# A two-layer streaming encoder on one core: Strassen's seven products for part of the second channel MLP

## The chip, the core and the metric

The kernel runs on one core of a Trainium2 chip. Its time is the device time of one execution in microseconds (us). Five engines work from queues of their own, each in order: TensorE (PE, with its weight loads PEld), VectorE (DVE), ScalarE (ACT), GpSimd (POOL) and SyncE (SP), which here issues nearly all DMAs.

## The reference

1024 prompt rows and 32 sample rows of 1024 channels go through two layers. Each layer has a mixer (a spatial gating unit in layer 0, a pooling mixer in layer 1) and a channel MLP (called the FFN), with an RMSNorm in front of and behind each of them and a modulation by the conditioning vectors (adaLN, "ada" in the kernel):

```
for i in range(DEPTH):                                  # 2 layers
    mod = silu(c) @ w_ada[i] + b_ada[i]
    sh1, sc1, gt1, sh2, sc2, gt2 = split(mod, 6)
    h = rmsnorm(x, g_norm[i, 0]) * (1 + sc1) + sh1
    mix = sgu_mixer(h) if i == 0 else pool_mixer(h)
    x = x + gt1 * rmsnorm(mix, g_norm[i, 1])
    h = rmsnorm(x, g_norm[i, 2]) * (1 + sc2) + sh2
    f = square(relu(h @ ffn_w_up[i])) @ ffn_w_down[i]   # 1024 -> 4096 -> 1024
    x = x + gt2 * rmsnorm(f, g_norm[i, 3])
```

All is float32. The pool mixer takes trailing means over 2, 4, 8 and 16 rows in four groups of 256 channels and multiplies each group with a 256 x 256 matrix.

## The kernel before

**Layout.** Channels lie on the partitions, in eight blocks of 128 (KB); rows are columns. The columns form three tiles: tiles 0 and 1 of 384 prompt rows, tile 2 of 256 prompt and 32 sample rows (288). `acc[t]` holds a tile's residual stream or the sum in the making, `hh[t]` and `hl[t]` its modulated input.

**Products.** Every factor is split into a high part and the rest: `wh` and `wl` for weights, `hh` and `hl` for the input, `fh` and `fl` for the hidden activations. A product is three matmuls, wh x hh, wh x hl and wl x hh (lines 847, 848 and 849). The split of a loaded weight block of 128 x 1024 is a copy on ACT (`wh`, line 404) and a difference on DVE (`wl`).

**The FFN.** It goes by chunks of 512 hidden channels, eight in a layer. One `ffn_item` is a chunk for one tile: four up blocks `pf` of 24 matmuls each, relu and square on ACT, the split into `fh` and `fl`, and later eight down blocks `pg` of 12 matmuls, each added into `acc[t]` by DVE. Part of the next item's up blocks goes ahead of the down part (`pending`, `flush`), so that TensorE has work while the hidden activations are made. `passes` (lines 305 to 312) lists the order: (layer, chunk, tiles that share the loaded weights). In layer 1 it is tile 0's chunks 0 to 3, tile 1's, tile 2's, then chunks 4 and 5 for all three, 6 and 7 for tiles 0 and 1, and 6 and 7 for tile 2.

**Weights.** One list, `stream`, holds all loads in order: weights and, between them, the pieces of `w_ada` (`some_ada`), whose sums DVE forms (`do_ada`, the tile aa). Each load lands in one of three `raw` buffers (line 377 issues it on SP), is split into two of sixteen slots, and a slot is free once its block has been used for the last time.

**The chain of a tile between the layers.** It is a generator, called a filler, whose steps `weave` puts between the blocks of the FFN, by a running count of TensorE's and DVE's time (`time["pe"]`, `time["dve"]`); `finish` forces what is left. In `to_pool` for tile t: the residual behind layer 0 (`residual`, with the tile re-read from DRAM as `xo_r` and stored again in `xd`), the norm and modulation, the window sums of the pool mixer (`win`), the products with its four matrices (`wg` loads, `pp` at line 1672, two blocks a group, copied into `acc[t]` by ACT and squared), the statistics (a matmul with ones, `pn`, then a reciprocal square root with one correction step: `sc`, `sm`, `r`, `q`), the residual behind the mixer (`mix_to_ffn`), its statistics, and the modulation: in `apply` DVE scales `acc[t]` in place, ACT writes `hh[t]` and DVE `hl[t]`. Names end with the tile in the code (`r_rp` of tile 1, `r_1x`), buffer numbers are left out in the profile. `run_ffn` calls `finish` on a tile's filler ahead of its chunk 0.

**The end.** `to_out` makes a tile's last residual, turns it by DVE transposes into `turned`, and stores it in 32 DMAs, 24 on SP and 8 on POOL.

Of the kernel before, what the change touches and what calls it, by code (L numbers as in the profile page):

```python
# [15 lines left out]
P = 128  # L16
D = 1024
KB = D // P
# [10 lines left out]
W_SLOTS = 16  # L29
RAW_SLOTS = 3  # L30
# [4 lines left out]
def tile_stream_encoder_step(  # L35
# [83 lines left out]
    vd = dram.tile([SEQ + DEC, SGU], F32, name="vd")  # L119

# [235 lines left out]
    wpos = {k: i for i, k in enumerate(worder)}  # L356
    wdone = set()
# [43 lines left out]
    def do_w(key, r):  # L401
# [4 lines left out]
        tt(out=wl, in0=r, in1=wh.bitcast(F32), op=ALU.subtract)  # L406

# [141 lines left out]
    def stream_ready():  # L549
        k = state["next"]  # L550
        if k >= len(stream):
            return False
        if stream[k][0] == "w":
            i = wpos[stream[k][1]] - W_SLOTS // 2
            return i < 0 or worder[i] in wdone
        return True

    def stream_step():
# [6 lines left out]
        if kind == "w":  # L565
            do_w(key, r)
        elif kind == "wide":
# [17 lines left out]
    def stream_waits():  # L585

        kind, key = stream[state["next"]][:2]
        if kind == "w":
# [834 lines left out]
    def ffn_item(p, t, after):  # L1423
# [88 lines left out]
    def mix_to_ffn(st, l):  # L1512
# [8 lines left out]
        yield from modulate(out[0], l, 2, 3)  # L1521
# [292 lines left out]
```

## Time and profile before

| | |
|---|---|
| Median of three runs | 2161.54 us (2161.33 to 2162.09) |
| The profiled execution | 2161.22 us |
| its span, first to last instruction | 2159.4 us |
| DVE busy | 1429.8 us (66%) |
| ACT busy | 971.0 us (45%) |
| POOL busy | 15.3 us (1%) |
| DMA, read and written | 312.96 MB, mean 145 GB/s |

The page is of the profiled execution. Busy times are the union of an engine's instructions, weight loads (PEld) overlap the matmuls. Durations of consecutive instructions of one engine can overlap, so the pace of a run of equal instructions is read from their starts. In rows of the timeline the first number is the start, the second the time, and "x2" says that two instructions in a row were joined. A matmul's name for its product is the tile that it writes (pf: up, pg: down, pp: pool mixer, pn: statistics).

### The profile page before, as it was taken

The numbers are of one execution on the slowest core, as the hardware profiler recorded it, in microseconds if no ns is written. First come the engines' busy times: TensorE is split into PE (matmuls) and PEld (weight loads), VectorE is DVE, ScalarE is ACT, GpSimd is POOL, SyncE is SP. The second block draws the span as 40 slices with busy tenths as digits, with TensorE's granted clock in tenths as the row PEclk, the third lists the DMA queues.
The fourth block names the chain that finished last, engine by engine and source line by source line (L and its number), as shares of the span: only waits on it lengthen the run. The fifth ranks groups of instructions, "written<-read, shape, count | busy, mean of one in ns | idle before, by whom it ended". The sixth has DMA issues, their size and how long they took to land.

```text
span 2159.4 us, 33252 instructions
## 1 busy us (share of the span) xinstructions
PE 2145.1 (99%) x13233; PEld 2076.5 (96%) x13233; DVE 1429.8 (66%) x2496; ACT 971.0 (45%) x1644; POOL 15.3 (1%) x34
## 2 busy tenths in 40 slices
PE   9999999999999999999999999999999999999998
PEld 6778999999999999999999999999999999999998
DVE  6787738457778549486757879869675554523377
ACT  5534322233456652323445566666554542313354
POOL 0000000000000000000000000000000000000001
PEclk9999999999999999999999999999999999999999
DMA  8487524253447454244645466565455552302255
GB/s 307 147 263 215 168 82 132 84 163 102 135 125 221 127 156 147 79 136 127 184 127 162 145 186 191 156 202 155 142 169 150 162 152 64 104 14 79 70 138 127
DMA packets 383152, 312.96 MB, mean 145 GB/s; under 512 B 39475, under 2 KB 346203, under 8 KB 382997
## 3 DMA queue, kind: packets, MB, share of 16 engines
q1 hardware_dynamic: 382324, 309.95, 47.5%
q8 instruction: 103, 1.69, 0.3%
q0 software_dynamic: 640, 0.88, 0.1%
q14 instruction: 53, 0.43, 0.1%
q10 hardware_dynamic: 32, 0.01, 0.0%
HBM read 278.95 MB, written 31.84 MB: 144 GB/s over the span
## 4 chain that ended last, share of the span: by engine, by line
PE 96%; DVE 2%; DMA 1%; ACT 1%; issue 0%; DVEq 0%; SPq 0%
PE pg L847 11%; PE pf L847 11%; PE pf L849 11%; PE pf L848 11%; PE pg L848 11%; PE pg L849 11%; PE po L847 3%; PE po L848 3%; PE po L849 3%; PE pu L847 3%; PE pu L849 3%; PE pu L848 3%; PE pv L874 2%; PE pv L875 2%; PE pv L876 2%; PE psp L1353 1%
## 5 line engine op out<-in xcount | busy, mean ns | idle before, releaser
L847 PE MATMUL pg<-fh,wh_dn 128*128 128x384 f32 (+1 forms) x1536 | 495.8, 323 | 0.0
L847 PE MATMUL pf<-hh,wh_up 128*128 128x384 f32 (+1 forms) x1536 | 494.4, 322 | 0.0
L848 PE MATMUL pf<-hl,wh_up 128*128 128x384 f32 (+1 forms) x1536 | 493.1, 321 | 0.0
L849 PE MATMUL pf<-hh,wl_up 128*128 128x384 f32 (+1 forms) x1536 | 492.9, 321 | 0.2 <-DVE wl_up L79 0.2
L848 PE MATMUL pg<-fl,wh_dn 128*128 128x384 f32 (+1 forms) x1536 | 492.6, 321 | 0.5 <-DVE fl L79 0.5
L849 PE MATMUL pg<-fh,wl_dn 128*128 128x384 f32 (+1 forms) x1536 | 492.5, 321 | 0.0
L79 DVE TENSOR_TENSOR wl_up<-raw,wh_up 128x1024 fp32r<-128x1024 f32 x152 | 185.5, 1221 | 164.5 <-ACT wh_up L404 164.5
L848 PEld LDWEIGHTS pg<-fl,wh_dn 128*128 128x128 f32 x1536 | 288.3, 188 | 1.6 <-DVE fl L79 0.8
L847 PEld LDWEIGHTS pg<-fh,wh_dn 128*128 128x128 f32 x1536 | 288.3, 188 | 1.5 <-ACT fh L1260 0.6
L849 PEld LDWEIGHTS pf<-hh,wl_up 128*128 128x128 f32 x1536 | 288.6, 188 | 0.5 <-DVE wl_up L79 0.5
L848 PEld LDWEIGHTS pf<-hl,wh_up 128*128 128x128 f32 x1536 | 288.3, 188 | 0.4
L847 PEld LDWEIGHTS pf<-hh,wh_up 128*128 128x128 f32 x1536 | 288.2, 188 | 0.4
L849 PEld LDWEIGHTS pg<-fh,wl_dn 128*128 128x128 f32 x1536 | 288.3, 188 | 0.0
L404 ACT ACTIVATE wh_up<-raw 128x1024 fp32r<-128x1024 f32 x152 | 161.2, 1060 | 278.2 <-PE pf L848 212.2
L79 DVE TENSOR_TENSOR acc<-acc,pg 128x384 f32<-128x384 f32 (+1 forms) x336 | 173.6, 517 | 146.9 <-PE pg L849 146.4
L404 ACT ACTIVATE wh_dn<-raw 128x1024 fp32r<-128x1024 f32 x152 | 160.8, 1059 | 204.0 <-PE pg L848 169.9
L79 DVE TENSOR_TENSOR wl_dn<-raw,wh_dn 128x1024 fp32r<-128x1024 f32 x152 | 185.7, 1223 | 83.8 <-ACT wh_dn L404 83.1
L79 DVE SCALAR_TENSOR_TENSOR aa<-raw,csil,aa 128x512 f32<-128x512 f32 (+1 forms) x364 | 203.1, 619 | 7.0 <-DMA raw<-in_w_ada_dram 6.3
L1435 ACT ACTIVATE r<-pf 128x384 f32<-128x384 f32 (+1 forms) x192 | 86.5, 450 | 202.0 <-PE pf L849 199.4
L79 DVE TENSOR_TENSOR fl<-r,fh 128x384 fp32r<-128x384 f32 (+1 forms) x192 | 99.8, 520 | 85.7 <-ACT fh L1260 84.6
L847 PE MATMUL pu<-hh,wh_u 128*128 128x384 f32 (+1 forms) x384 | 125.8, 328 | 0.0
L847 PE MATMUL po<-ush,wh_o 128*128 128x384 f32 (+1 forms) x384 | 123.6, 322 | 0.0
(280 smaller groups left out, 2920.3 us busy)
## 6 DMA issues: line engine op xcount, KB each, us to landing
raw<-in_ffn_w_up_dram SPq DMA_DIRECT2D x152, 512.0 KB, 3.9
raw<-in_ffn_w_down_dram SPq DMA_DIRECT2D x152, 512.0 KB, 3.4
raw<-in_w_ada_dram SPq DMA_DIRECT2D x96, 512.0 KB, 4.5
raw<-in_sgu_w_in_dram SPq DMA_DIRECT2D x40, 512.0 KB, 4.5
xd<-acc SPq DMA_DIRECT2D x8, 1536.0 KB, 6.9
raw<-in_sgu_w_out_dram SPq DMA_DIRECT2D x24, 512.0 KB, 3.9
xo_r<-xd SPq DMA_DIRECT2D x32, 384.0 KB, 3.3
vd<-vt SPq DMA_DIRECT2D x32, 256.0 KB, 4.5
```

Source lines behind the costliest of these rows:

```text
L79: return op(out, *args, **kw)
L404: act(out=wh, in_=r, func=AF.Copy)
L847: mm(ps[:, :n], wh, rh, start=i == 0, stop=False)
L848: mm(ps[:, :n], wh, rl, start=False, stop=False)
L849: mm(ps[:, :n], wl, rh, start=False, stop=i == last)
L874: mm(ps[:m, :], a_h, wh[:, o : o + 512], start=k == 0, stop=False)
L875: mm(ps[:m, :], a_h, wl[:, o : o + 512], start=False, stop=False)
L876: mm(ps[:m, :], a_l, wh[:, o : o + 512], start=False, stop=k == KB - 1)
L1353: mm(sp[:, c * P : (c + 1) * P], vl[:, c, k * P : (k + 1) * P], wr[:, c * P : (c + 1) * P], start=True, stop=True,)
L1435: act(out=r[:, :n], in_=ps[:, :n], func=AF.Relu)
```

## The change

For tiles 0 and 1 together, the up products of chunks 4 to 7 of layer 1 are computed by Strassen's scheme in the variant with fewer additions (Winograd's). A product of a 2 x 2 block matrix of weights (two halves of the input blocks, two of the hidden blocks) with a 2 x 2 block matrix of inputs (the same halves, and the two tiles as columns) takes seven block products and no eighth. The weights' sums and differences are formed on DVE for each loaded item (`do_s`, kind "s" in the stream). The inputs' are formed once, by a filler `sums_of_columns`, from copies of the modulated tiles, `md`, that are now stored in DRAM; the buffers for them, and the spares for hidden activations, are gathered from tiles that are not in use then, among them `hh` and `hl` of tile 2. In `combined_item` the seven products go to two accumulators each half, with copies on ACT and additions on DVE between them. The down products stay as they were.

The order of layer 1 becomes: tile 0's chunks 0 and 1, tile 1's chunks 0 and 1, chunk 2 for tiles 0 and 1, chunk 3 for tiles 1 and 0, chunks 4 to 7 combined, then all eight chunks of tile 2. Tile 2's mixer and residual still run early; its modulated input is scaled and stored in `md`, and `late_modulation` reads it back behind the combined chunks. The loads of `w_ada` that lay in layer 1 now lie in tile 0's chunks 6 and 7 of layer 0. Slots are counted by their use from shortly ahead of the combined chunks on.

```diff
...
+COMBINED = 4
...
+    md = [dram.tile([P, KB, n], F32, name=f"md{t}") for t, n in enumerate(ncol)]
...
-        for j in range(4):
+        if n in combined:
+            for i in range(2):
+                f0 = c * 512 + i * 256
+                for q in range(2):
+                    stream.append(
+                        (
+                            "s",
+                            ("up", n, i, q),
+                            ffn_w_up[l][q * 512 : (q + 1) * 512, f0 : f0 + 256].rearrange(
+                                "(k p) f -> p k f", p=P
+                            ),
+                            (4, 256),
+                        )
+                    )
+        for j in range(0 if n in combined else 4):
...
-    passes += [(1, c, [t]) for t in every for c in range(4)]
-    passes += [(1, c, every) for c in range(4, 6)]
-
-    passes += [(1, c, every[:-1]) for c in (6, 7)]
-    passes += [(1, c, [NT - 1]) for c in (6, 7)]
+    pair = every[:-1]
+    passes += [(1, c, [t]) for t in pair for c in (0, 1)]
+    passes += [(1, c, pair if c != 7 - COMBINED else pair[::-1]) for c in range(2, 8)]
+    combined = range(len(passes) - COMBINED, len(passes))
+    passes += [(1, c, [NT - 1]) for c in range(8)]
...
-            some_ada(12 if len(tiles) > 1 else 4 if c in (4, 5) and tiles == every[:1] else 0)
-        elif len(tiles) > 1:
-            some_ada(4)
-    some_ada(99)
-
-    worder = [s[1] for s in stream if s[0] == "w"]
+            some_ada(12 if len(tiles) > 1 else 4 if c >= 4 and tiles == every[:1] else 0)
+    assert not rest
...
+    def do_s(key, r):
+        p, i, q = key[1:]
+        a, b, sh, sl = (
+            work.tile([P, 1024], F32R, tag="W", bufs=W_SLOTS, name=f"{x}_up_{p}_{i}_{q}")
+            if q == 0 or x != "wl"
+            else None
+            for x in ("wh", "wl", "sh", "sl")
+        )
+        a = fours(a)
+        sh4, sl4 = fours(sh), fours(sl)
+        if q == 0:
+            b = fours(b)
+            shared[p, i] = a, b
+            parts = [(a[:, 0:2], b[:, 0:2]), (a[:, 2], b[:, 2])]
+        else:
+            x, z = shared.pop((p, i))
+            parts = [(a[:, 0:2], a[:, 2:4]), (x[:, 3], z[:, 3])]
+        x = quarters(r)
+        srcs = [x[:, :, :, 0, :].rearrange("p a b f -> p b a f"), x[:, :, 1, 1, :]]
+        for (hi, _), src in zip(parts, srcs):
+            act(out=hi, in_=src, func=AF.Copy)
+        s = scratch[:, :1024]
+        v = fours(s)
+        tt(out=v[:, 0], in0=x[:, :, 0, 1, :], in1=x[:, :, 1, 1, :], op=ALU.add)
+        tt(out=v[:, 2], in0=x[:, :, 0, 0, :], in1=x[:, :, 0, 1, :], op=ALU.subtract)
+        tt(out=v[:, 1], in0=v[:, 0], in1=x[:, :, 0, 0, :], op=ALU.subtract)
+        tt(out=v[:, 3], in0=x[:, :, 1, 0, :], in1=v[:, 1], op=ALU.subtract)
+        act(out=sh, in_=s, func=AF.Copy)
+        for (hi, lo), src in zip(parts, srcs):
+            tt(out=lo, in0=src, in1=hi.bitcast(F32), op=ALU.subtract)
+        tt(out=sl, in0=s, in1=sh.bitcast(F32), op=ALU.subtract)
+        (first, second) = parts
+        witem[key] = [
+            (first[0][:, 0], first[1][:, 0]),
+            (first[0][:, 1], first[1][:, 1]),
+            second,
+        ] + [(sh4[:, n], sl4[:, n]) for n in range(4)]
...
+            if i < wtight:
+                return i < W_SLOTS // 2 or worder[i - W_SLOTS // 2] in wdone
+            used = sum(cost(key) for key in worder[:i] if key not in wdone)
+            return used + cost(worder[i]) <= w_cap[0]
...
+        if p + 1 == combined[0] and t == 1:
+            finish("ffn1_2")
+            fillers.append(("sums", sums_of_columns()))
...
+    def combined_item(p, after):
+        l, c, tiles = passes[p]
+        n = ncol[0]
+        spare = sums["spare"]
+        hid = {t: [None] * 4 for t in tiles}
+        made = [0]
+
+        def parts():
+            i = made[0]
+            made[0] += 1
+            if i < 5:
+                return tuple(t_hid(x, f"f{x}{l}_{c}_{i}") for x in "hl")
+            return spare[i - 5], spare[i - 2]
+
+        def finish_block(r, ps, t, j):
+            if ps is not None:
+                act(out=r[:, :n], in_=ps[:, :n], func=AF.Relu)
+            else:
+                act(out=r[:, :n], in_=r[:, :n], func=AF.Relu)
+            act(out=r[:, :n], in_=r[:, :n], func=AF.Square)
+            a, b = parts()
+            split(a, b, r, n)
+            hid[t][j] = (a, b)
...
+        def blocks(i):
+            w = [need_w(("up", p, i, q)) for q in range(2)]
+
+            def product(ps, first, a, b):
+                tick(12 * (0.004 + n / 2265.0))
+                for k in range(4):
+                    q, m = divmod(k, 2)
+                    wh, wl = (x[:, m, :] for x in w[q][a])
+                    bh, bl = b(k)
+                    for x, (u, v) in enumerate(((wh, bh), (wh, bl), (wl, bh))):
+                        mm(
+                            ps[:, :n],
+                            u,
+                            v,
+                            start=first and k == 0 and x == 0,
+                            stop=k == 3 and x == 2,
+                            skip_group_check=True,
+                        )
+
+            def column(t, odd):
+                return lambda k: (hh[t][:, 2 * k + odd, :], hl[t][:, 2 * k + odd, :])
+
+            def summed(j):
+                return lambda k: sums["parts"][j, k]
+
+            def copy(name, ps, out=None):
+                out = t_m(name) if out is None else out
+                act(out=out[:, :n], in_=ps[:, :n], func=AF.Copy)
+                return out
+
+            def add(x, ps):
+                tt(out=x[:, :n], in0=x[:, :n], in1=ps[:, :n], op=ALU.add)
+
+            pa = ps_up(f"pf{p}_{i}a")
+            product(pa, True, 0, column(0, 0))
+            u1 = copy(f"u1_{p}_{i}", pa)
+            yield
+            pb = ps_ms(f"pf{p}_{i}b")
+            product(pb, True, 1, column(0, 1))
+            add(u1, pb)
+            finish_block(u1, None, 0, 2 * i)
+            yield
+            product(pa, False, 4, summed(1))
+            u2 = copy(None, pa, temp(i))
+            pc = ps_ms(f"pf{p}_{i}c")
+            product(pc, True, 5, summed(2))
+            product(pa, False, 3, summed(0))
+            u4 = copy(None, pa, temp(2))
+            add(u4, pc)
+            finish_block(u4, None, 1, 2 * i + 1)
+            yield
+            product(pa, False, 6, column(1, 1))
+            finish_block(t_m(f"r_{p}_{i}"), pa, 1, 2 * i)
+            product(pc, False, 2, summed(3))
+            add(u2, pc)
+            finish_block(u2, None, 0, 2 * i + 1)
+            for q in range(2):
+                w_finish(("up", p, i, q))
+            yield
+
+        def down(t):
+            st = None
+            for d in range(KB):
+                ps = ps_dn(f"pg{l}_{c}_{t}_{d}")
+                wh, wl = need_w(("dn", p, d // 2))
+                terms = []
+                for j in range(4):
+                    o = j * 256 + (d % 2) * P
+                    a, b = hid[t][j]
+                    terms.append((wh[:, o : o + P], wl[:, o : o + P], a[:, :n], b[:, :n]))
+                products(ps, n, terms)
+                accumulate(t, d, ps, False)
+                if d == 0 and after is not None:
+                    st = Stat(t, f"rf{l}_{t}")
+                if after is not None:
+                    st.square(d)
+                if t == tiles[-1] and d % 2 == 1:
+                    w_finish(("dn", p, d // 2))
+                weave(d % 2)
+            if after is not None:
+                after(st)
+
+        first, second = blocks(0), blocks(1)
+        flush()
+        next(first)
+        next(first)
+        next(first)
+        weave()
+        next(second)
+        next(first)
+        weave()
+        next(second)
+        next(second)
+        weave()
+        next(second)
+        if after is not None:
+            w_cap[0] = W_SLOTS
+            fillers.appendleft(("ffn1_2", late_modulation(NT - 1)))
+        weave()
+        for t in tiles:
+            down(t)
...
+        got = []
+        yield from out[0].finish(got)
+        if t < NT - 1:
+            yield from apply(t, l, 2, 3, got[0])
+            nc.sync.dma_start(md[t], acc[t][:, :, HALO:])
+            return
...
+        for i in range(4):
+            t1, t3, t2 = (temp(m) for m in range(3))
+            t4 = t_m(f"sums_m{i}")
+            nc.sync.dma_start(t1, md[0][:, 2 * i, :])
+            nc.sync.dma_start(
+                scratch[:, 1408:2176].rearrange("p (a n) -> p a n", a=2), md[1][:, 2 * i : 2 * i + 2, :]
+            )
+            nc.sync.dma_start(t4, md[0][:, 2 * i + 1, :])
+            yield 3.0
+            tt(out=t1, in0=t3, in1=t1, op=ALU.subtract)
+            tt(out=t3, in0=t2, in1=t3, op=ALU.subtract)
+            tt(out=t2, in0=t2, in1=t1, op=ALU.subtract)
+            tt(out=t4, in0=t4, in1=t2, op=ALU.subtract)
+            yield True
...
+    def late_modulation(t):
+        a = acc[t][:, :, HALO:]
+        nc.sync.dma_start(a, md[t])
+        hh[t] = room("h", t, f"hh1_2_{t}", F32R)
+        hl[t] = room("l", t, f"hl1_2_{t}", F32R)
+        yield 4.0
...
+            if p in combined:
+                finish("sums")
+                combined_item(p, after if c == 7 else None)
+                continue
...
```

More of the change, by code (lines that the diff above doesn't have):

```diff
@@ L406, in do_w, with cost, quarters, temp @@
         tt(out=wl, in0=r, in1=wh.bitcast(F32), op=ALU.subtract)
+    w_cap = [W_SLOTS - 2]
+    def cost(key):
+        return 2 if len(key) != 4 or key[0] != "up" else 4 - key[3]
+    def quarters(x):
+        return x.rearrange("p (a b h f) -> p a b h f", a=2, b=2, h=2)
+    scratch = acc[NT - 1].rearrange("p k n -> p (k n)")
+    def temp(i):
+        return scratch[:, 1024 + 384 * i : 1408 + 384 * i]
+    def fours(x):
+        return x.rearrange("p (s a f) -> p s a f", s=4, a=2)
+    shared = {}
+    def do_s(key, r):
[35 more added lines that the diff above has]
+        ] + [(sh4[:, n], sl4[:, n]) for n in range(4)]
     ada_acc = {}
@@ L566, in stream_step @@
             do_w(key, r)
+        elif kind == "s":
+            do_s(key, r)
         elif kind == "wide":
@@ L1520, in mix_to_ffn @@
         need_ada(l, 4)
-        yield from modulate(out[0], l, 2, 3)
+        if l == 0:
+            yield from modulate(out[0], l, 2, 3)
+            return
[4 more added lines that the diff above has]
+            nc.sync.dma_start(md[t], acc[t][:, :, HALO:])
+            return
+        for k in range(KB):
+            for c0, w, v in segs[t]:
+                a = A(t, k, c0, w)
+                stt(
+                    out=a,
+                    in0=a,
+                    scalar=coef[:, l, 2, v, k : k + 1],
+                    in1=got[0][:, c0 : c0 + w],
+                    op0=ALU.mult,
+                    op1=ALU.mult,
+                )
+            yield False
@@ new lines, in late_modulation @@
+    def late_modulation(t):
[4 more added lines that the diff above has]
+        yield 4.0
+        for k in range(KB):
+            for c0, w, v in segs[t]:
+                c = slice(c0, c0 + w)
+                b = shift[:, 1, 1, k, v : v + 1]
+                act(out=hh[t][:, k, c], in_=a[:, k, c], func=AF.Identity, bias=b, scale=1.0)
+                stt(
+                    out=hl[t][:, k, c],
+                    in0=a[:, k, c],
+                    scalar=b,
+                    in1=hh[t][:, k, c].bitcast(F32),
+                    op0=ALU.add,
+                    op1=ALU.subtract,
+                )
+            yield False
```

69 lines of the change are left out of this document (65 added, 4 removed).

## The prediction

> **What bounds the kernel now.** I read the page's busy shares first, then its chain of waits and the granted clock, then the matmuls in the timeline.
>
> ```profile
> PE 2145.1 (99%) x13233; PEld 2076.5 (96%) x13233; DVE 1429.8 (66%) x2496; ACT 971.0 (45%) x1644; POOL 15.3 (1%) x34
> PE 96%; DVE 2%; DMA 1%; ACT 1%; issue 0%; DVEq 0%; SPq 0%
> core 0: 2159.4 us, clock 0.998
> ```
>
> TensorE is busy 99% of the span, and 96% of the chain that ended last is TensorE. So a matmul taken away is worth its own pace, as long as TensorE finds the next one ready. By the same token every wait put into TensorE's queue is paid in full: there is almost no idle time that could swallow it.
>
> The pace comes from the starts of consecutive matmuls, not from the duration column, since matmuls overlap.
>
> ```profile
> 1413.72 0.33 PE L847 MATMUL pg<-fh,wh_dn 128*128 128x384 f32 x1
> ...
> 1418.92 0.33 PE L847 MATMUL pg<-fh,wh_dn 128*128 128x384 f32 x1
> ...
> 1350.03 0.30 PE L847 MATMUL pg<-fh,wh_dn 128*128 128x288 f32 x1
> ...
> 1350.43 0.29 PE L847 MATMUL pg<-fh,wh_dn 128*128 128x288 f32 x1
> ```
>
> The first pair, of 384 columns, is 30 rows apart: 5.20/30 = 0.173 us. The second pair, of 288 columns (the third tile), is three apart: 0.133 us. One FFN chunk of tile 0 or 1 is 192 matmuls, 33.3 us, half of it up and half down; one of tile 2 is 25.5 us.
>
> Next the stretches around the place where layer 0 ends and layer 1 begins (columns: TensorE, its weight loads, DVE, ACT, POOL, clock, DMA share, GB/s):
>
> ```profile
> 1102.00:1164.00 62.00, 62.00 (x360) 62.00 (x359) 39.24 (x57) 34.51 (x53) 0.00 (x0) 1.00 0.39 117
> 1164.00:1287.00 123.00, 123.00 (x693) 118.75 (x693) 95.06 (x142) 67.29 (x106) 0.00 (x0) 1.00 0.59 176
> 1287.00:1375.00 88.00, 88.00 (x658) 88.00 (x657) 72.77 (x109) 56.68 (x93) 0.00 (x0) 1.00 0.64 192
> 1373.00:1435.00 62.00, 62.00 (x369) 59.88 (x369) 51.30 (x84) 40.55 (x73) 0.00 (x0) 1.00 0.52 152
> 1435.00:1496.00 61.00, 61.00 (x342) 58.35 (x341) 50.68 (x87) 39.78 (x69) 0.00 (x0) 1.00 0.60 188
> ```
>
> TensorE is full in all five. DVE has 23 us free in the first (tile 0's chunks 6 and 7 of layer 0) and some 28, 15, 11 and 10 us in the others. In the last two, tile 0's four chunks of layer 1, DVE also carries the pool mixer, the residual and the modulation of tiles 1 and 2. They are covered by 4 x 33.3 = 133 us of matmuls.
>
> **What goes away.** Each of the last four chunks has its up products for tiles 0 and 1 as 7 x 2 x 4 x 3 = 168 matmuls in place of 2 x 96 = 192. That is 24 x 4 = 96 fewer in the program's TensorE list, and no added ones: 96 x 0.173 = **16.6 us** off. All of it is on the path.
>
> **The combined chunks (chunks 4 to 7).** The costs come from these groups (busy, mean ns):
>
> ```profile
> L79 DVE TENSOR_TENSOR wl_up<-raw,wh_up 128x1024 fp32r<-128x1024 f32 x152 | 185.5, 1221 | 164.5 <-ACT wh_up L404 164.5
> L404 ACT ACTIVATE wh_up<-raw 128x1024 fp32r<-128x1024 f32 x152 | 161.2, 1060 | 278.2 <-PE pf L848 212.2
> L79 DVE TENSOR_TENSOR acc<-acc,pg 128x384 f32<-128x384 f32 (+1 forms) x336 | 173.6, 517 | 146.9 <-PE pg L849 146.4
> L79 DVE TENSOR_TENSOR fl<-r,fh 128x384 fp32r<-128x384 f32 (+1 forms) x192 | 99.8, 520 | 85.7 <-ACT fh L1260 84.6
> L1435 ACT ACTIVATE r<-pf 128x384 f32<-128x384 f32 (+1 forms) x192 | 86.5, 450 | 202.0 <-PE pf L849 199.4
> ```
>
> A weight item of the new kind has on DVE four operations on 256 elements, differences of 512 and 256 and one of 1024. The trace has 1.22 us at 1024 and 0.52 at 384; between them I estimate 0.65 for 512 and 0.42 for 256: 4 x 0.42 + 0.65 + 0.42 + 1.22 = 4.0 us, four per chunk. With four down splits (4.9), 16 accumulations (8.3), 8 splits of the hidden blocks (4.2) and 6 additions of products (3.1) DVE has about 36 us in a chunk of 168 + 192 matmuls, 62.4 us. ACT: items 4 x 2.0, down copies 4.2, three operations of 0.45 to 0.5 on 8 blocks and 6 copies of products, about 27 us. Neither is a bound. Each copy out of an accumulator has twelve matmuls (2.1 us) on the other accumulator before the first is written again, against 0.45 for the copy. What shows is the end of the up part: the last block needs addition, relu, square, copy and difference, 0.52 + 4 x 0.45 to 0.5, about 2.6 us, before the last terms of the first down block can run, with some 19 matmuls (3.3 us) in between. In order behind weight items it may be late by 0 to 2 us each time. I take 0.5 per chunk: **2 us** (0 to 8).
>
> **The new order, and the chain of tile 1.** Now tile 0 has only chunks 0 and 1 before tile 1 needs its modulated input: 66.7 us of cover in place of 133. Beside that, all the remaining ada loads go into layer 0, four each in tile 0's chunks 6 and 7.
>
> ```profile
> L79 DVE SCALAR_TENSOR_TENSOR aa<-raw,csil,aa 128x512 f32<-128x512 f32 (+1 forms) x364 | 203.1, 619 | 7.0 <-DMA raw<-in_w_ada_dram 6.3
> ```
>
> There are 96 loads, so 203.1/96 = 2.1 us of DVE each, 17 us for eight. DVE's free 23 us in 1102 to 1164 shrink to 6, and what was done there goes later. The program's TensorE list of the changed kernel shows the result: half of tile 1's pool mixer (pp of groups 2 and 3) stands behind the last down block of tile 0's chunk 1, and then come only the statistics (pn) of the mixer and of the residual, eight small transposes and tile 1's first up block. No other matmul is left to run in between. So this chain, covered before, lies open. Its steps in the trace of before, where it ran among others' work:
>
> ```profile
> 1452.61 2.58 PE pp L1672 x8
> ...
> 1455.63 0.57 ACT L1676 ACTIVATE acc<-pp,vec 128x384 f32<-128x384 f32 x1
> ...
> 1459.38 0.61 DVE L79 SCALAR_TENSOR_TENSOR sm_rp<-sq_rp,eps,sc_rp 128x384 fp32r<-128x384 f32 x1
> ...
> 1463.11 0.55 DVE L79 SCALAR_TENSOR_TENSOR r_rp<-q_rp,r_rp 128x384 f32<-128x384 f32 x1
> ...
> 1464.71 1.14 DVE L79 SCALAR_TENSOR_TENSOR acc<-acc,coef,r_rp 128x384 f32<-128x384 f32 x2
> ...
> 1466.23 0.95 DVE L79 TENSOR_TENSOR acc<-acc,xo_r 128x768 f32<-128x768 f32 x1
> 1467.11 0.61 DVE L79 SCALAR_TENSOR_TENSOR acc<-acc,coef,r_rp 128x384 f32<-128x384 f32 x1
> ...
> 1472.56 0.95 DVE L79 TENSOR_TENSOR sq_r_1x<-sq_r_1x 128x768 f32<-128x768 f32 x1
> ...
> 1480.46 0.60 ACT L725 ACTIVATE sc_r_1x<-sq_r_1x,eps 128x384 fp32r<-128x384 f32 x1
> ...
> 1489.70 0.49 ACT L744 ACTIVATE r_r_1x<-pn_r_1x 128x384 f32<-128x384 f32 x1 [0.68 <-PE pn_r_1x L740]
> 1490.22 0.53 ACT L745 ACTIVATE q_r_1x<-r_r_1x 128x384 f32<-128x384 f32 x1
> ...
> 1493.69 1.14 DVE L79 SCALAR_TENSOR_TENSOR acc<-acc,coef,r_r_1x 128x384 f32<-128x384 f32 x2
> 1494.34 1.15 ACT L820 ACTIVATE hh<-acc,shift 128x384 fp32r<-128x384 f32 x2 [0.27 <-DVE acc L79]
> ```
>
> Call T the end of tile 0's last down block. Two groups of pp take 2 x 2.58 = 5.2 us. From the end of pp (1455.2) to the end of r_rp (1463.66) it took 8.5 us there, of which I estimate 1.7 as waiting behind a down copy ahead of the scale, a split ahead of sm and two small operations ahead of r_rp: 6.8, so T + 12.0. The residual is 8 operations at 0.53 (the pair of 1.14 less overlap), 4 additions of xo_r and 2 of squares at 0.88 each (0.95 long, the next starts 0.88 after it): 9.4, T + 21.4. Then one square (0.85) and two additions (0.95, 0.55), scale and mean (0.60 + 0.61), the statistics matmuls (0.5), the reciprocal root on ACT (0.49 + 0.53) and on DVE (0.54 + 0.55), some 6.2 together: T + 27.8 with 0.2 of hand-over. One modulation on DVE and hh on ACT (0.6 each): T + 29.1. In its way also stands the store of the residual, which the modulation overwrites and so waits for; it is issued at T + 21.4.
>
> ```profile
> xd<-acc SPq DMA_DIRECT2D x8, 1536.0 KB, 6.9
> xo_r<-xd SPq DMA_DIRECT2D x32, 384.0 KB, 3.3
> raw<-in_ffn_w_up_dram SPq DMA_DIRECT2D x152, 512.0 KB, 3.9
> out_dram<-turned SPq DMA_DIRECT2D x48, 48.0 KB, 2.1
> ```
>
> 6.9 us later is T + 28.3, half a microsecond behind the chain: T + 29.6. The matmuls in it (5.2 of pp, about 1.5 of statistics and transposes) would have run anyway: **22.9 us** of TensorE idle (18 if each hand-over is free and the store beats the chain, 28 if weight splits stand in DVE's queue ahead of the squares). Then 16 operations of 0.53 feed 48 matmuls of 0.173, 8.5 against 8.3 us, so no more is lost there.
>
> **The matmuls behind a long idle.** At the program's start, out of idle, they are slower:
>
> ```profile
> 1.36 5.49 PE L928 MATMUL warm<-ones 128*128 128x512 f32 x12 [1.36 <-DVE ones L129]
> 2152.00:2156.00 4.00, 0.00 (x0) 0.00 (x0) 3.90 (x5) 0.00 (x0) 0.00 (x0) 0.50 0.62 241
> ```
>
> Twelve of 512 columns take 5.49 us, 0.46 each, where 512 x 0.173/384 = 0.231 would be the pace: 2.7 us lost in 5.5. The granted clock falls to 0.50 where TensorE has nothing to do. Whether a 15 us hole does the same in the middle no row shows: 0 to 2.7 us, of which I take half, **1.4**.
> The Trainium skill, "TensorE: Matmul & The Clock Gate", Part 1, speaks against the change here: it says that an idle window of about 3.4 us halves the clock, and that about 3.4 us of work restores it. An estimate from that page is 1.7 us for the hole, and the sum would be 0.3 longer; the start's doubled matmul time agrees with it, though the granted clock is 1.00 in those rows.
>
> **Smaller waits.** Ahead of T, DVE has window sums of tile 1, tile 2's residual and chunk 1's splits in one queue, about 40 us of work in tile 0's chunk 1 (33.3 us, and the pp in it). If the splits of that chunk come late, TensorE waits at its down part: 0 to 5, take **2**. The sums of columns for Strassen's operands run as a filler during chunk 3: four rounds, each with loads of 192 to 384 KB (3.3 us by the xo_r row), four differences and eight splits, about 8 us a round through one shared buffer, in 67 us of matmuls of two tiles, most of it in the later one: DVE about 42 of 50 us; take **1.5** (0 to 6). At the switch to tile 2, its modulation writes a buffer that holds spares of the combined blocks until the last of them is read: one difference of 0.4, one matmul hand-over, **0.7** (0 to 2). In tile 2's eight chunks, now last, 48 stores of tiles 0 and 1 share SP's queue with 64 weight loads. A store waits for the eighth before it (2.1 us), loads queue behind it; the program's list shows up and down blocks interleaved where weights are expected late. DMA needs 4 MB in 25.5 us, which 1287 to 1375 shows to be possible at full TensorE (192 GB/s there): **2** (0 to 8).
>
> **Sum.** Against the profiled execution: 2159.4 span + 1.8 around it = 2161.2 (0.3 under the median of the runs). 2161.2 - 16.6 + 2 + 22.9 + 1.4 + 2 + 1.5 + 0.7 + 2 = **2177.1 us**.
>
> **Rivals.**
> *The saving alone (faster).* If tile 1's chain were done by T, only 16.6 goes and 0 to 8 of small waits come: 2145 to 2153. For it: DVE had 10 to 11 us free in each of the two stretches. Against: pp of groups 2 and 3 stands behind T in TensorE's queue, and everything after hangs on it. 0.06.
> *The hole is half as long (no change).* If the residual's chain goes at the rate of its longest engine alone, some 15 us, and the small waits are nil, 2161.2 - 16.6 + 15 + 1 = 2161. Against: it is one chain in order, ACT to DVE to TensorE, and I could shorten only hand-overs. 0.10.
> *Weights late in tile 2's chunks (much slower).* SP's queue holds the loads behind stores, and stores wait for the transposes, which wait for TensorE. Two tiles of 24 stores are three rounds of 2.1 us each; where the loaded weights (sixteen slots, eight items, so at most one chunk ahead) last for less than 6.3 us, TensorE waits, and the residual's xo_r loads (3.3) add to it: 2 x (6.3 + 3.3) less the 2 taken gives 17 more, 2194. For it: a single chunk of tile 2 has 25.5 us for eight loads, in place of 92 for three tiles. Against: in 1287 to 1375 TensorE is full at the same load. 0.20.
> *DVE becomes the bound in chunk 3 and the combined chunks*, if operations on strided quarters cost twice my estimate: 4 x 4.0 more per chunk, 52 of 62.4, with the late last block at 2 us each and the sums at 6: 2177 + 6 + 4.5 = 2188. 0.12.
> The forecast has the remaining 0.52.
>
> **How the numbers follow.** The predicted time is the forecast's 2177. Its own range is 2168 to 2186, from the hole's 18 to 28 and the small waits. The range for 8 in 10 reaches up to the two slower rivals and down to the edge of the half hole: 2164 to 2195. About 0.2%, 4.3 us, is what can be told from no change, so faster means under 2157.2: the first rival, with little of the second, 0.07. Same, to 2165.8: most of the second and the forecast's edge, 0.11. Slower 0.82.
>
> **What would show it.** TensorE's idle should be one hole of 20 to 28 us ahead of tile 1's first up block, ended by hh or hl, with DVE and ACT taking turns in it; its releaser in the chain of waits would be DVE with a share near 3% rather than 2. TensorE's busy time should be lower by 16.6. In the combined chunks idle before the first down block should be under 2 us each. Tile 2's chunks should show waits on weights of a few microseconds in all. Wrong it would be if TensorE's list stood still for less than 15 us there (then faster or same), or if the rows of waits named DMA or weights with over 10 us.

## The result and the profile after

| | before | changed |
|---|---|---|
| median | 2161.82 us (2161.33 to 2162.60, 4 runs) | 2186.20 us (2184.45 to 2187.31, 4 runs) |
| ratio | | 1.0112 (1.0094 to 1.0129) |
| span of the profiled execution | 2159.4 us | 2185.4 us |
| forecast | | 2177.1 us, range 2164 to 2195 |

The page of the changed kernel and, from its waits, the longest ones of TensorE (us in total, times, longest):

```profile
PE 2141.9 (98%) x13137; PEld 2063.5 (94%) x13137; DVE 1491.8 (68%) x2649; ACT 1000.0 (46%) x1716; POOL 15.4 (1%) x34
PE 89%; DVE 5%; DMA 3%; ACT 2%; issue 1%; DVEq 0%; ACTq 0%
...
PE pn_r_1x L816 <- ACT sc_r_1x L801: 15.0, 1, 15.0
PE pn_rp L816 <- ACT sc_rp L801: 2.8, 1, 2.8
PE pg L925 <- DVE wl_dn L80: 2.3, 2, 1.2
PE pg L924 <- DVE fl L80: 1.9, 3, 0.9
PE pf L923 <- ACT r L1511: 1.7, 2, 1.4
...
PE pn_rf L816 <- ACT sc_rf L801: 1.5, 1, 1.5
...
PE pf L923 <- ACT hh L896: 1.3, 1, 1.3
PE cacheT L1880 <- DVE q_r_1x L80: 1.1, 1, 1.1
...
PE pg L923 <- ACT sums_l L1336: 0.9, 1, 0.9
PE pf L924 <- DVE hl L80: 0.8, 1, 0.8
```

Before, the waits of TensorE were some 4 us in all. Now one alone is 15.0, and the chain that ended last has 5% of DVE, 3% of DMA and 2% of ACT in place of 2, 1 and 1. TensorE's idle time rose from 2159.4 - 2145.1 = 14.3 to 2185.4 - 2141.9 = 43.5 us, by 29.2. Its busy time fell by 3.2 only, though 96 matmuls are gone: a matmul of 384 columns counts as 0.33 us of busy time where the next one starts after 0.173, and one at a slow pace counts in full, so short waits vanish in the busy time and starts have to be read.

The hole itself, in the chain of waits (start, us, what), from the last down block of tile 0's chunk 1 on:

```profile
1460.85 4.53 PE pp L1993 x14
...
1468.86 1.35 PE pn_rp L816 x2
...
1471.90 0.57 DVE r_rp L80
...
1476.02 2.88 DVE acc L80 x4
...
1484.52 0.62 ACT sc_r_1x L801
...
1488.39 0.57 DVE r_r_1x L80
```

These are the steps that the prediction walked in the trace of before, now with nothing else between them: DVE and ACT take turns, and TensorE has only the statistics and eight small transposes in it. Then the matmuls behind the hole, and the granted clock over it (start, us, matmul; windows: TensorE, weight loads, DVE, ACT, POOL, clock, DMA share, GB/s):

```profile
1460.69 5.32 PE L1993 MATMUL pp<-acc,wg 128*128 128x384 f32 x16
...
1490.31 1.01 PE L923 MATMUL pf<-hh,wh_up 128*128 128x384 f32 x2 [1.29 <-ACT hh L896]
...
1492.05 0.52 PE L923 MATMUL pf<-hh,wh_up 128*128 128x384 f32 x1
...
1496.07 0.33 PE L925 MATMUL pf<-hh,wl_up 128*128 128x384 f32 x1
1496.25 0.33 PE L923 MATMUL pf<-hh,wh_up 128*128 128x384 f32 x1
```

```profile
1470.00:1485.00 15.00, 0.20 (x1) 0.00 (x0) 12.16 (x18) 4.87 (x7) 0.00 (x0) 0.50 0.24 75
1490.00:1495.00 5.00, 4.69 (x14) 4.25 (x15) 5.00 (x11) 2.98 (x6) 0.00 (x0) 0.50 0.00 0
1495.00:1500.00 5.00, 5.00 (x29) 5.00 (x28) 2.63 (x5) 1.14 (x2) 0.00 (x0) 0.95 0.47 175
```

From the fourth matmul to 1495.25 the starts lie 0.32 us apart (the first three steps take 0.45 to 0.49), from 1495.5 on 0.17 to 0.18: 15 matmuls in 5.2 us, where 0.173 each would be 2.6. The granted clock is 0.50 through the hole and for 5 us behind it.

Where the time went, from the starts of matmuls (each less its pace of 0.173 or 0.132): the hole 29.6 - 6.7 of its own matmuls = 22.9, 15 slow matmuls behind it 5.2 - 2.6 = 2.6, waits at chunk 1's first down block 1.6, the sums 0.9, the combined chunks 3.7, the switch to tile 2 2.6, tile 2's chunks 5.7 in gaps of 0.4 and more. That is 40.0, less 16.6 saved 23.4; the spans of the two profiled executions are 26.0 apart (the medians 24.4), so 2.6 us have no place in this list.

### The profile page after: what moved, and what is told of

The parts are those of the page before. It is cut to its first block, busy times and chain, and to the rows that moved or that the text cites. A ratio compares the mean times of both kernels' runs of the same rounds, so it can differ in the third digit from the quotient of the medians.

```text
span 2185.4 us, 33239 instructions
## 1 busy us (share of the span) xinstructions
PE 2141.9 (98%) x13137; PEld 2063.5 (94%) x13137; DVE 1491.8 (68%) x2649; ACT 1000.0 (46%) x1716; POOL 15.4 (1%) x34
## 4 chain that ended last, share of the span: by engine, by line
PE 89%; DVE 5%; DMA 3%; ACT 2%; issue 1%; DVEq 0%; ACTq 0%
PE pg L923 10%; PE pg L925 10%; PE pg L924 10%; PE pf L923 8%; PE pf L924 8%; PE pf L925 8%; PE po L923 3%; PE po L924 3%; PE po L925 3%; PE pu L923 3%; PE pu L925 3%; PE pu L924 3%; PE pv L951 2%; PE pv L950 2%; PE pv L952 2%; PE pf_0a L1588 2%
## 5 line engine op out<-in xcount | busy, mean ns | idle before, releaser
L923 PE MATMUL pg<-fh,wh_dn 128*128 128x384 f32 (+1 forms) x1440 | 463.6, 322 | 1.4 <-ACT fh L1336 1.0
L925 PE MATMUL pg<-fh,wl_dn 128*128 128x384 f32 (+1 forms) x1440 | 460.2, 320 | 2.3 <-DVE wl_dn L80 2.3
L923 PE MATMUL pf<-hh,wh_up 128*128 128x384 f32 (+1 forms) x1280 | 409.7, 321 | 3.4 <-ACT r L1511 1.7
L924 PE MATMUL pf<-hl,wh_up 128*128 128x384 f32 (+1 forms) x1280 | 408.2, 319 | 0.8 <-DVE hl L80 0.8
L925 PE MATMUL pf<-hh,wl_up 128*128 128x384 f32 (+1 forms) x1280 | 408.0, 319 | 0.1
L80 DVE TENSOR_TENSOR wl_up<-raw,wh_up 128x1024 fp32r<-128x1024 f32 (+1 forms) x160 | 177.1, 1114 | 131.6 <-ACT wh_up L419 130.7
L923 PEld LDWEIGHTS pf<-hh,wh_up 128*128 128x128 f32 x1280 | 240.6, 188 | 5.0 <-ACT r L1511 2.3
L924 PEld LDWEIGHTS pf<-hl,wh_up 128*128 128x128 f32 x1280 | 240.8, 188 | 2.0 <-DVE hl L80 1.5
L925 PEld LDWEIGHTS pf<-hh,wl_up 128*128 128x128 f32 x1280 | 241.2, 188 | 1.0 <-DVE wl_up L80 1.0
L925 PE MATMUL pu<-hh,wl_u 128*128 128x384 f32 (+1 forms) x384 | 123.4, 321 | 0.0
```

The costliest lines, as they stand in the source:

```text
L80: return op(out, *args, **kw)
L923: mm(ps[:, :n], wh, rh, start=i == 0, stop=False)
L924: mm(ps[:, :n], wh, rl, start=False, stop=False)
L925: mm(ps[:, :n], wl, rh, start=False, stop=i == last)
```

## The experiments

All times are medians with their lowest and highest run, and ratios to the kernel before, run on the same chip.

**More cover for tile 1's chain** (2168.49 us, 2166.53 to 2171.47; ratio 1.0027, 1.0017 to 1.0038).

```diff
-    passes += [(1, c, [t]) for t in pair for c in (0, 1)]
-    passes += [(1, c, pair if c != 7 - COMBINED else pair[::-1]) for c in range(2, 8)]
+    passes += [(1, c, [t]) for t in pair for c in (0, 1, 2)]
+    passes += [(1, c, pair if c != 7 - COMBINED else pair[::-1]) for c in range(3, 8)]
```

> Tile 0 gets three chunks of its own ahead of tile 1 (then tile 1 three, chunk 3 for the pair, 4 to 7 combined as in the change). One chunk more of cover, 33.3 us. My theory: the hole is tile 1's chain lying open behind two chunks, so it shrinks from 26 us (29.6 from the end of the last down block to the first up block, less 5.2 and 1 of work, plus 2.5 of slow matmuls) to 4 to 9 us, since the last statistics of the chain still stand behind the last down block in TensorE's list: 2163 to 2172. Rival, that DVE is short of time there whatever the cover: the hole only moves, 2180 or more.

17.7 us came back, with one chunk of cover. What is left of the hole, in this kernel's timeline of TensorE:

```profile
1504.02 0.28 PE L1924 MATMUL stT_p<-ident,acc 128*16 128x128 f32 x1 [2.77 <-ACT acc L1901]
...
1506.06 1.01 PE L923 MATMUL pf<-hh,wh_up 128*128 128x384 f32 x2 [1.16 <-ACT hh L896]
```

A wait of 2.8 and one of 1.2, and again matmuls 0.32 apart until 1511.3. So the cover sets the hole, and DVE was not short of time as such.

**The order alone** (2194.53 us, 2194.14 to 2194.84; ratio 1.0152, 1.0137 to 1.0167). The order of chunks, the stores of `md` and the late modulation stay, the up products are ordinary ones.

```diff
-    combined = range(len(passes) - COMBINED, len(passes))
+    pairs = range(len(passes) - COMBINED, len(passes))
+    combined = ()
...
-        if p + 1 == combined[0] and t == 1:
-            finish("ffn1_2")
-            fillers.append(("sums", sums_of_columns()))
+        if p + 1 == pairs[0] and t == 1:
+            finish("ffn1_2")
+        if p == pairs[-1] and t == 0:
+            fillers.appendleft(("ffn1_2", late_modulation(NT - 1)))
```

> The new order of chunks, the stores and the late modulation of tile 2, the ada loads in layer 0, but ordinary up products in chunks 4 to 7 (and no sums of columns). My theory: the combined chunks give all 16.6 us of their 96 matmuls and lose about 1 by a late last block, so without them the time is 2186.2 + 16.6 - 1 - 1 (sums of columns) = 2201 (2197 to 2205). Rival: the combined chunks give back much of their saving in copies and sums: 2196 or less.

The combined products are worth 8.3 us, half of the 16.6 that was counted: the theory's 2197 is missed, the rival's "2196 or less" holds. One period of a chunk, from the first up matmul to that of the next, first in the changed kernel, then in this one:

```profile
1705.13 0.33 PE L1588 MATMUL pf_0a<-hh,wh_up 128*128 128x384 f32 x1
...
1768.16 0.33 PE L1588 MATMUL pf_0a<-hh,wh_up 128*128 128x384 f32 x1
```

```profile
1706.75 0.33 PE L924 MATMUL pf<-hh,wh_up 128*128 128x384 f32 x1
...
1773.31 0.33 PE L924 MATMUL pf<-hh,wh_up 128*128 128x384 f32 x1
```

66.56 us against 63.03 where 360 x 0.1733 = 62.4 was the count: each combined chunk keeps 3.5 of its 4.2. Of the rest, the sums take 0.9, the last chunk's first down block 1.1, and at the switch to tile 2 TensorE waits 0.8 for hl and 1.5 for tile 1's statistics, which have no gap in this kernel. That leaves 16.6 - 2.6 - 0.9 - 1.1 - 2.3 = 9.7; where the other 1.4 went stays open (3.0 by the profiled executions, whose spans are 6.7 apart).

**The ada loads back in layer 1** (2181.61 us, 2180.86 to 2182.04; ratio 1.0092, 1.0077 to 1.0107).

```diff
-            some_ada(12 if len(tiles) > 1 else 4 if c >= 4 and tiles == every[:1] else 0)
+            some_ada(12 if len(tiles) > 1 else 4 if c in (4, 5) and tiles == every[:1] else 0)
+        elif n < combined[0] and len(tiles) > 1:
+            some_ada(4)
```

> The eight ada loads go back from layer 0's chunks 6 and 7 to layer 1 (four with chunk 2, four with chunk 3); all else as changed. TensorE's list then has all of tile 1's pool mixer ahead of the last down block of tile 0's chunk 1, but the residual behind the mixer still behind it. My theory: the hole is some 19 us in place of 26, and chunk 3 has more DVE work: 2178 to 2183. Rival, that the moved ada work is the cause of the hole: 2165 or less. Rival, that it has no part in it: 2185 to 2188.

4.6 us, as far as pp and its statistics could move ahead of the last down block. This kernel's waits of TensorE still have the residual's statistics:

```profile
PE pn_r_1x L818 <- ACT sc_r_1x L803: 15.4, 1, 15.4
```

So the moved ada work accounts for a small part, as the theory had it, and the missing chunk of cover for most of the rest: the two gains, 17.7 and 4.6, add up to what both bring together further down (22.3).

**TensorE kept at work in the hole** (first try 2189.00 us, 2185.47 to 2189.67; second 2184.63 us, 2183.65 to 2188.13). Matmuls into an accumulator that nobody reads, 66 ahead of the residual's statistics in the first, 102 ahead and 18 behind in the second:

```diff
+        if t == 1:
+            pw = ps_dn("warm_hole")
+            for _ in range(102):
+                mm(pw[:, :384], onesr, hh[0][:, 0, :], start=True, stop=True)
         yield from out[0].finish(got)
+        if t == 1:
+            pw = ps_dn("warm_gap")
+            for _ in range(18):
+                mm(pw[:, :384], onesr, hh[0][:, 0, :], start=True, stop=True)
```

> 66 matmuls of 384 columns into an unused accumulator are put into the hole, between the statistics of the mixer and those of the residual, about 14 us of the 15 in which TensorE sat idle; all else as changed. My theory: the first 17 matmuls behind the hole, 0.32 us apart in the changed kernel, go at 0.173, so 2.5 us less: 2183 to 2184.5. Rival, that they are slow for another reason (their inputs come at that rate): no change, 2185.5 to 2187.

> The earlier try of filling the hole left 7 us of it idle, and the matmuls behind it were still slow. Here 102 matmuls go in ahead of the residual's statistics and 18 behind them, so that TensorE has work nearly to the first up block. My theory: no slow matmuls behind the hole, the first six steps of the up block at the pace of their inputs (about 1.06 for six), 2.5 us less at most: 2183.5 to 2186, and the trace shows starts 0.17 to 0.18 apart. Rival, that their inputs set the pace: starts 0.32 apart as before.

In the first, 16 of the added matmuls ran ahead of the mixer's statistics, the last ended by 1478.5, and TensorE was idle for 6.9 us: the starts 0.32 us apart came back, for 9 matmuls in place of 15 (the expectations say 17), and the time was 2.8 us higher, which neither the theory nor the rival had and which stays unexplained (its profiled execution, 2185.47, is the fastest of the four). In the second there was no such idle stretch, and the up block began like this:

```profile
1488.17 2.42 PE L1738 MATMUL warm_gap<-hh,ones 128*128 128x384 f32 x13
...
1493.18 0.34 PE L925 MATMUL pf<-hh,wl_up 128*128 128x384 f32 x1
1493.35 0.34 PE L923 MATMUL pf<-hh,wh_up 128*128 128x384 f32 x1
```

```profile
1491.00:1496.00 5.00, 4.17 (x28) 3.69 (x26) 5.00 (x11) 3.50 (x7) 0.00 (x0) 1.00 0.00 0
```

From the fourth matmul on the starts are 0.17 apart, at a clock of 1.00, with the same inputs from DVE, and the first 15 take 3.3 us in place of 5.2. So 1.9 us of the slow matmuls come from the idle time, the other 0.7 from waiting for inputs. The time, 1.6 us lower, fits that but is within the spread of both kernels.

**The stores of tiles 0 and 1 on POOL's queue** (2191.56 us, 2189.71 to 2193.28; ratio 1.0130, 1.0116 to 1.0144).

```diff
-                    (nc.gpsimd if q == 3 else nc.sync).dma_start(
+                    (nc.gpsimd if q == 3 or t < NT - 1 else nc.sync).dma_start(
```

> The 48 stores of tiles 0 and 1 that went through SP's queue go through POOL's, as the other 16 do; all else as changed. My theory of the waits in tile 2's chunks (some 7 us of late weights): the weight loads stand behind the stores in SP's queue. Then 3 to 5 us go: 2181 to 2183.5. Rival: SP's queue is not what holds them; the loads land late because the DMA engines share their time with the stores (4.4 to 4.7 us for a weight load there in place of 3.5 to 4.0) and three raw buffers give no more lead: 2185 to 2188.

Neither: 5.4 us more. The reason is in this kernel's timeline of DVE and of POOL:

```profile
2034.45 2.37 DVE L1700 STREAM_TRANSPOSE xlast_h<-xlast_l 128x1024 f32<-128x1024 f32 x2 [15.46 <-DMA out_dram<-turned]
```

```profile
2029.88 1.28 POOL L2084 DMA_DIRECT2D out_dram<-turned  x2 [1.04 <-issue]
2032.18 1.29 POOL L2084 DMA_DIRECT2D out_dram<-turned  x2 [1.03 <-issue]
```

POOL issued two stores every 2.3 us. DVE stood 15.5 us at a transpose of tile 2's last rows, whose destination has the buffer that those stores still read; weight splits and fl were queued behind it, and TensorE waited 8.9 us for fl. The weights themselves came earlier, as the theory had it: in the changed kernel ACT, which makes the high part of each weight block, waits 22.3 us for weight loads from 1985 to 2140; here it does so once, for 13.8 us, while DVE is held and frees no raw buffer.

**Both, in steps.** Three chunks each with the eight ada loads in tile 1's chunks 1 and 2 took 2163.86 us (2162.60 to 2167.47; ratio 1.0006, 0.9997 to 1.0015). With them in tile 1's chunk 2 and in chunk 3, 2160.33 us (2158.15 to 2162.54; ratio 0.9988, 0.9979 to 0.9997). The order of chunks is that of the three chunks above; the ada loads of the second:

```diff
-            some_ada(12 if len(tiles) > 1 else 4 if c >= 4 and tiles == every[:1] else 0)
+            some_ada(12 if len(tiles) > 1 else 4 if c in (4, 5) and tiles == every[:1] else 0)
+        elif c == 2 and tiles == every[1:2] or c == 3:
+            some_ada(4)
```

> Three chunks of tile 0, three of tile 1, chunk 3 for the pair, 4 to 7 combined, and the eight ada loads in tile 1's chunks 1 and 2 in place of layer 0's 6 and 7. TensorE's list then has tile 1's last statistics 36 matmuls ahead of the end of tile 0's chunk 2. My theory: the hole is closed (the 26 us of it, of which the three chunks alone had left 8 to 9): 2159 to 2163, the rest of the saving being eaten by the combined chunks' late last block (0.65 each), the switch to tile 2 (3) and its late weights (7). Rival: the chain of tile 1 is followed by that of tile 2, and the wait only moves on: 2166 or more.

> As the kernel with three chunks each and the ada loads back in layer 1 (2163.9), but with four ada loads in tile 1's chunk 2 and four in chunk 3 in place of its chunks 1 and 2, where tile 2's pool mixer runs. My theory: the wait of 2.4 us on tile 2's statistics (and 0.9 on its first matrix) goes, the rest stays: 2159.5 to 2162.5. Rival: the ada work meets the sums of columns in chunk 3 and the wait returns there: 2163 to 2166.

The hole of tile 1 is closed in both; the first is 0.9 us above its stated range. There tile 2's chain had become the next one, with the wait below, which is gone in the second:

```profile
PE pn_rp L818 <- ACT sc_rp L803: 2.4, 1, 2.4
```

The first with the stores on POOL took 2171.63 us (2167.74 to 2173.42): 7.8 more, which neither of its two cases had: the same transpose holds DVE for 15.3 us.

> The one before with the 48 stores on POOL's queue. If SP's queue holds the weights back, 3 to 5 us less than it: 2155 to 2160. If not, the same within 1 us.

**Tile 2's late weights.** The kernel of 2160.33 us, leaving out the 48 stores of tiles 0 and 1 on SP, took 2161.40 us (2158.97 to 2162.68); with 32 stores on each of SP and POOL 2159.97 us (2158.16 to 2161.26).

> The same, leaving out the 48 stores of tiles 0 and 1 on SP's queue (three quarters of their output isn't written). My theory: the weights of tile 2's chunks come late because stores and weight loads run at once; without the stores the some 6 us of waits there go to 1 or less: 5 us less than with them. Rival: eight chunks of one tile of 288 columns outrun the weight loads by themselves: at most 1 us less.

> The same with the stores halved between SP's and POOL's queues (32 and 32 in place of 48 and 16). Earlier, with all on POOL, one came every 1.15 us, and a transpose into a buffer that the stores still read held DVE for 15 us. Halved, POOL needs 16 x 1.15 = 18 us for a tile, SP half of its time: if SP's queue holds the loads, 2 to 4 us less than the kernel with three quarters on SP; if DVE waits for POOL's stores, 2 to 8 us more.

By their times neither says anything (5 us less was expected of the first). Their traces do. First the waits of TensorE for weights in the kernel with all stores, then DVE in the one without those on SP, then in the halved one:

```profile
PE pg L927 <- DVE wl_dn L80: 2.3, 2, 1.2
```

```profile
1973.04 1.25 DVE L1702 STREAM_TRANSPOSE xlast_h<-xlast_l 128x1024 f32<-128x1024 f32 x1 [6.65 <-DMA out_dram<-turned]
```

```profile
1984.31 1.25 DVE L1702 STREAM_TRANSPOSE xlast_h<-xlast_l 128x1024 f32<-128x1024 f32 x1 [4.69 <-DMA out_dram<-turned]
```

Without SP's stores no wait of TensorE in tile 2's chunks is for a weight split, and none over 0.3 us comes after 1985; a weight load lands in 3.4 to 4.0 us (median) where it takes 4.1 to 4.8 with them, and ACT's waits for loads from 1960 to 2110 fall from 22.8 to 3.2 us. But DVE now comes to its transpose at 1966.4 in place of 1987.2, when stores of tile 0 on POOL's queue (8 of its 32) still read that buffer: it is held for 6.7 us, and TensorE waits 5.1 us for fl. One loss hid the other. If that is so, moving the turned tiles out of that buffer must show it:

```diff
-            turned = room("h", t, f"turned{t}")
+            turned = room("l" if t else "h", 1, f"turned{t}")
...
-                    (nc.gpsimd if q == 3 else nc.sync).dma_start(
+                    (nc.gpsimd if q > 1 else nc.sync).dma_start(
```

> As the kernel with halved stores (2160.0), but the turned tiles 0 and 1 lie in the buffers of tile 1's input (free by then) in place of those into which DVE transposes tile 2's last rows. My theory: with the stores spread over two queues the weights come in time, and what was left of waits in tile 2's chunks (5.4 us by 2010 in that run) came from DVE, held 4.7 us by a transpose that waited for stores on POOL's queue. Then 3 to 5 us go: 2155 to 2157. Rival: the weights of tile 2's chunks are late anyway, and the waits come back later in those chunks: 2159 to 2161.

2155.25 us (2152.45 to 2159.02; ratio 0.9966, 0.9954 to 0.9978). It is below the kernel before by 0.34%. Five stretches of 26 us in tile 2's chunks of this kernel, then of the changed one, in both from the second chunk of tile 2 on, which the stores of tiles 0 and 1 overlap:

```profile
1980.00:2006.00 26.00, 23.84 (x178) 23.40 (x177) 21.30 (x30) 12.78 (x21) 7.58 (x14) 1.00 0.80 220
2006.00:2032.00 26.00, 25.93 (x183) 25.76 (x184) 11.23 (x18) 8.53 (x15) 3.62 (x6) 0.94 0.56 150
2032.00:2058.00 26.00, 26.00 (x198) 26.00 (x198) 18.97 (x24) 14.95 (x22) 0.00 (x0) 1.00 0.79 221
2058.00:2084.00 26.00, 26.00 (x198) 26.00 (x198) 16.06 (x22) 15.13 (x23) 0.00 (x0) 1.00 0.67 197
2084.00:2110.00 26.00, 26.00 (x198) 26.00 (x197) 15.35 (x21) 13.77 (x23) 0.00 (x0) 1.00 0.57 169
```

```profile
1988.00:2014.00 26.00, 26.00 (x198) 26.00 (x198) 15.02 (x27) 11.58 (x22) 3.73 (x6) 1.00 0.55 140
2014.00:2040.00 26.00, 25.55 (x189) 24.86 (x189) 21.68 (x31) 13.18 (x20) 3.72 (x6) 1.00 0.72 204
2040.00:2066.00 26.00, 23.69 (x175) 22.93 (x173) 11.26 (x17) 8.75 (x14) 0.00 (x0) 1.00 0.64 155
2066.00:2092.00 26.00, 26.00 (x197) 25.76 (x195) 18.32 (x23) 15.22 (x23) 0.00 (x0) 1.00 0.78 218
2092.00:2118.00 26.00, 24.08 (x178) 23.40 (x177) 17.30 (x23) 16.83 (x25) 0.00 (x0) 1.00 0.76 222
```

A full stretch has 198 matmuls. This kernel lacks 35 in the first two stretches, 4.6 us at 0.132, and is full from 2032 on; the changed kernel lacks 53 in the five, 7.0 us. DVE is no longer held by a transpose. What is left is at 2003 to 2009:

```profile
2003.33 1.06 ACT L421 ACTIVATE wh_up<-raw 128x1024 fp32r<-128x1024 f32 x1 [1.41 <-DMA raw<-in_ffn_w_up_dram]
2004.29 0.43 ACT L1338 ACTIVATE fh<-r 128x288 fp32r<-128x288 f32 x1
```

```profile
2004.77 0.40 PE L925 MATMUL pg<-fh,wh_dn 128*128 128x288 f32 x1 [1.32 <-ACT fh L1338]
...
2006.71 0.44 PE L925 MATMUL pg<-fh,wh_dn 128*128 128x288 f32 x1
2006.95 0.44 PE L926 MATMUL pg<-fl,wh_dn 128*128 128x288 f32 x1
```

It is a late weight load at second hand: ACT waits for the load, fh stands behind that copy, and TensorE waits 1.3 us for fh and then 0.9 for fl. Behind these waits its matmuls start 0.24 us apart in place of 0.132, until 2009.1, at a granted clock of 0.50. So the rival had a part of it: ACT still waits 27.2 us for weight loads from 1960 to 2110, with 32 stores on SP's queue.

## Why the prediction came out as it did

The direction and the main cause were right. The time lies in the stated range, 9.1 us above the forecast and at the upper edge of the forecast's own range (2168 to 2186). The terms below are 7.5 us more than forecast; the other 1.6 have no place. Its steps:

*The saving, 16.6.* The count was right, the period of a chunk shows 4.2 less 0.65.

*The hole, 22.9.* Right to a few tenths, with TensorE idle for 15.0 + 2.8 + 1.3 + 1.1 = 20.2 us in it. T is 1460.69; r_rp ended at T + 11.8 (forecast 12.0), the last addition of xo_r at T + 21.3 (21.4), r_r_1x at T + 28.3 (27.8), the first up matmul started at T + 29.6 (29.6). That the store of the residual would end half a microsecond behind the chain was not so: it landed after 5.8 us, not 6.9, and the modulation started as soon as r_r_1x was there. The chain itself was half a microsecond longer than its 27.8, so that the 29.6 came out to the tenth is luck. DVE's share of the chain of waits is 5%, not the 3% named as a sign. And DVE's free 23 us in 1102 to 1164 shrank to 16.3, not to 6, so the moved ada loads press on DVE less than the working has it; put back, they gain 4.6 us, one more chunk of cover 17.7. The half-long hole and the rival that has the saving alone are out.

*The slow matmuls, 1.4.* 2.6, of which 1.9 by the idle time; the row of the program's start, 2.7 lost, was the right one, not half of it. The granted clock in the hole's rows (0.50) agrees with the Trainium skill, "TensorE: Matmul & The Clock Gate", Part 1, that idle time halves the clock; its 3.4 us until it is restored are 5.2 here.

*The wait at chunk 1, 2, and the sums, 1.5.* 1.6 and 0.9.

*The combined chunks, 2.* 3.7: 0.65 a chunk as a small lengthening of every period, and 1.1 at the last chunk's first down block, where TensorE waits for the last hidden block. The 0.5 each was a little low.

*The switch to tile 2, 0.7, and tile 2's chunks, 2.* These two terms were mis-sized, at 2.6 and 5.7 or more. At the switch only the buffer's hand-over was counted; DVE's sixteen modulation steps, 4.55 us in one piece (0.8 of wait), and tile 1's last statistics behind them (1.5) were not. In tile 2's chunks the cause, weights late beside the stores of tiles 0 and 1, was seen and priced too low: with the 48 stores on SP's queue ACT waits 22.8 us for loads, without them 3.2. How much of this is the order in SP's queue and how much the transfers in flight together (a load lands in 4.1 to 4.8 us beside them, in 3.4 to 4.0 without) is not separated: all 64 on POOL's queue leave one wait, but they also come one per 1.15 us; 32 on each queue leave 27.2 us. The stores' hold on a buffer that DVE needs was not seen; it costs the changed kernel nothing (0.2 us) and showed only when stores were moved or left out. The rival of late weights, 2194, had the place right and the size too large.

*TensorE's busy time* was to fall by 16.6 and fell by 3.2; that sign was a wrong one to name, since slow matmuls and short waits are not counted as idle.

*DVE as the bound* is out: 34.3 us busy in a combined chunk of 63.0 (forecast 36 of 62.4).

## What to carry to other kernels

A reordering that takes cover from a chain is priced by walking that chain with the durations of the old trace: from the point where TensorE's list has nothing left in between, every step came out within half a microsecond over 29.6. A saving in the products is worth its count only if the order that it asks for keeps every chain covered; here one chunk more ahead of tile 1 and 17 us of DVE work put elsewhere turned 1.1% slower into 0.1% faster. Where moving a transfer to another queue changes nothing, look at who holds its source buffer before calling the queue innocent.

## What was not expected of the hardware

POOL issued a store of 48 KB every 1.15 us (two in 2.3). After idle stretches of 2.8 and 1.2 us with little work between, as after the 15 us hole, matmuls of 384 columns ran 0.32 us apart for about 5 us; after 1.3 and 0.9 us with one matmul between, matmuls of 288 columns ran 0.24 us apart for 2.6. There 2.2 us of waits cost another 1.2 in slow matmuls.
